# A slot order of its own for pair 5 in the RWKV-7 scan, with the value products and the output projection's first steps at other places

## The chip, the core and the metric

The kernel runs on one core of a Trainium2 chip. The metric is device time in microseconds (us) of one execution, the median of several. A core has five engines with an instruction queue each, and each queue runs strictly in its order: PE (TensorE, matrix products into PSUM banks), ACT (ScalarE), DVE (VectorE), POOL (GpSimd) and SP (SyncE), which here issues all DMA transfers. An instruction that waits for a semaphore holds up everything behind it in its queue.

## The reference, cut to what matters

The trunk has two layers on 512 tokens of 1024 channels. Each is a half-step SwiGLU FFN, a token mixer, and a second half-step FFN, each followed by a residual and a layer norm. Layer 0 mixes by neighbourhood attention, layer 1 by a bidirectional RWKV-7 scan. The change lies in that scan.

```python
def rwkv7_bidir(x, mix, w_rkv, ..., w_out):
    ...
    r = xr @ w_rkv[0]
    k = xk @ w_rkv[1]
    v = xv @ w_rkv[2]
    ...
    def step(state, inp):
        r_t, w_t, k_t, v_t, a_t, b_t = inp
        sa = jnp.einsum('zbhij,zbhj->zbhi', state, a_t)
        state = state * w_t[..., None, :] + sa[..., None] * b_t[..., None, :] + v_t[..., None] * k_t[..., None, :]
        return state, jnp.einsum('zbhij,zbhj->zbhi', state, r_t)

    _, ys = lax.scan(step, jnp.zeros((2, B, H, N, N), f32), xs)
    y = (ys[:, 0] + ys[::-1, 1]).transpose(1, 0, 2, 3)
    ...
    return ((y + bonus) * g).astype(x.dtype) @ w_out
```

There are 16 heads of 64 channels and two directions. The last line is the output projection: 512 x 1024 outputs, summed over 1024 channels. The layer adds `ALPHA * x` and normalises.

## The kernel before, in words

The scan treats two heads at a time: eight pairs, 0 to 7, of 128 channels each. A pair's sequence is cut in `NC` = 8 chunks of 64 tokens, and `chain` carries the state from chunk to chunk. One chunk takes four groups of small matmuls on PE with copies on other engines between them: `c` (line 1429), a copy to `wr` on ACT (1430), the first part of `y` (1433), `c` with `az` (1441), two copies to `vt` on ACT (1442, 1443), `m` (1447), and a product on DVE (1449) that gives the next chunk's `vt`. That chain of engines is serial; `outputs` (1460) and other pairs' work stand between its parts on PE.

Everything is written as Python generators, one per job and pair, and a program is made slot by slot: the slot of pair n runs `chain(n)`, and beside it the preparation of later pairs and the finishing of earlier ones. The order inside a slot is a string of letters in the table `SEQ`, one letter for one step of a generator; PE, ACT and DVE run in exactly the recorded order (`MANUAL_SCAN`). SP and POOL are ordered by the scheduler at build time, which places each DMA by its own estimate of when the DMA's waits end; on the chip that order is fixed. A slot without an entry of its own in `SEQ` takes entry 0; before the change, pair 5's slot did so. The letters that matter here:

- `c` chain, `d` outputs of the pair of the slot (5).
- `v` (`values`, line 1306): for pair n+2 = 7. The first step loads 512 KB of weights into the tile `wv`; the eight others each multiply one of 8 channel blocks of the activations `xv` with it into a bank "a" and after the eighth ACT copies the result. One such step is two matmuls (`wide`, line 990), which the profile shows as four records.
- `g0`, `g1` (`grams`): products of pair 7's tiles `ar` and `bk`, and DMAs that copy parts of `ar` into state tiles (`xs<-ar`, line 1292). `t0`, `t1` (`tails`, line 1302): transposes of `bk`.
- `k` (`inverted`, line 1380): pair 6's inverted blocks, a transpose on DVE and eight DMAs `az<-qd` (line 1385). `b` bonus; `x`, `e`, `n`, `j`, `i` other finishing and preparing steps.
- `o` (`outs`, line 1471): the output projection over the first `EARLY` = 5 channel blocks. It loads rows of `w_out`, 512 KB for a block, and the finished scan outputs of earlier pairs back from DRAM into `xv`, in place of the activations there. Then come 8 accumulations (4 token tiles x 2 column halves) of 5 steps each, so 40 steps. Each step is again one `wide`. The blocks of `w_out` have no room of their own: `w[0]` takes over `wv`, and `w[1]` to `w[4]` take over the two buffers of `ar` and the two of `bk`, oldest first, when pair 7 is done with them. `w[5]` to `w[7]` take over state tiles (line 1492 loads two of them).

Before, the `o` steps begin in the slot of pair 6, 26 of them, and 14 follow in the slot of pair 7. In the slot of pair 5 the last of the value steps stands almost at the slot's end.

Of the kernel before, what the change touches and what calls it, by code (L numbers as in the profile page):

```python
# [18 lines left out]
P = 128  # L19
# [23 lines left out]
CH = 64  # L43
NC = S // CH
# [940 lines left out]
class Scan:  # L985
# [485 lines left out]
    def outs(self):  # L1471

        nc = self.nc
        rows = lambda ap, k: ap[k * P : (k + 1) * P, :]
        w = [self.tile("wv", [P, ND, P]).rearrange("p a b -> p (a b)")]
        w += [self.tile(n, [P, NC, 2, CH], 2).rearrange("p a b c -> p (a b c)") for n in ("ar", "ar", "bk", "bk")]
        w += [self.units[i][0].rearrange("p a b c d -> p (a b c d)") for i in (2, 4, 3)]
        self.w, self.left = w, [rows(self.dram["x"], t) for t in range(NT)]
        for i in range(EARLY - 1):
            nc.sync.dma_start(self.xv[:, i, :], self.dram["o"][:, i, :])  # L1480
            nc.sync.dma_start(w[i], rows(self.w_out, i))
        for n, (t, h) in enumerate((t, h) for t in range(NT) for h in range(2)):
            hs = slice(h * 512, (h + 1) * 512)
            x = self.tile(("e", "e2", "th")[n % 3], [P, S], 2)
            nc.sync.dma_start(x, rows(self.dram["x"], t)[:, hs])
            acc = self.k.bank("ag"[n % 2])
            for i in range(EARLY):
                if n == 0 and i == EARLY - 1:
                    nc.sync.dma_start(self.xv[:, i, :], self.dram["o"][:, i, :])
                    nc.sync.dma_start(w[i], rows(self.w_out, i))  # L1490
                    for c in range(EARLY, ND - 1):
                        nc.sync.dma_start(w[c], rows(self.w_out, c))
                self.wide(acc, self.xv[:, i, t * P : (t + 1) * P], w[i][:, hs], i == 0, i == EARLY - 1)
                if i < EARLY - 1:
                    yield
            nc.vector.scalar_tensor_tensor(x, x, ALPHA, acc, ALU.mult, ALU.add)
            nc.sync.dma_start(rows(self.dram["x"], t)[:, hs], x)
            self.stored += 1
            self.reload()
            yield  # L1500
# [200 lines left out]
```

## Time and profile before

| what | value |
|---|---|
| median of three runs | 2250.02 us |
| lowest and highest run | 2245.41, 2254.24 us |
| the profiled execution's own time | 2249.58 us |
| its span, first to last instruction | 2247.8 us |
| mean granted clock of PE | 0.983 |

In the trace the slot of pair 5 lies from 1746.3 to 1784.0 us on PE, that of pair 6 to 1830.8, and that of pair 7 to 1857.4. A row of the timeline gives start and duration in us, engine, line, operation and tiles, the number of merged records, and in square brackets how long the engine had been idle and what released it. "SPq" rows are DMAs as SP issues them; when the data lands is in the DMA view. Records of PE are pipelined and overlap by some tens of ns.

### The profile page before, as it was taken

To read this page: it belongs to the slowest core of one execution; us is meant where nothing else is said; L and a number is where in the kernel's file an instruction comes from. 1 tells how busy PE (TensorE), PEld (TensorE's weight loads), DVE (VectorE), ACT (ScalarE), POOL (GpSimd) and SP (SyncE) were. 2 spreads that over 40 slices of the span, in tenths; PEclk is the share of its full clock that TensorE was granted. 3 is DMA by queue.
4 is the path that set the end of the run, shared out by engine and by line. 5 is a ranking of instruction groups with operands and counts; after the bars stand their busy time and mean duration, and the time that the engine had idled before them with its cause. 6 is when DMAs were issued, how large, how long until landed. Compare 5 with 4: busy or idle time off the path is not lost.

```text
span 2247.8 us, 35130 instructions
## 1 busy us (share of the span) xinstructions
PE 2169.0 (96%) x13784; PEld 1707.8 (76%) x13784; DVE 1068.3 (48%) x1549; ACT 973.8 (43%) x1706; POOL 1425.7 (63%) x1237
## 2 busy tenths in 40 slices
PE   8999999999999999999999988699999998999998
PEld 7888888887888888888888875435667656888886
DVE  2333356276423333743333698425778645232345
ACT  3333345376333333443333435336777633333333
POOL 6878855554487886588887433144776722888854
PEclk9999999999999999999999999799999999999999
DMA  6444463432344445354444534764454642544443
GB/s 199 143 145 145 143 229 97 135 89 91 103 141 150 145 141 174 132 181 137 141 141 132 196 123 155 268 162 117 126 137 111 206 149 94 159 141 141 141 169 122
DMA packets 350497, 328.82 MB, mean 146 GB/s; under 512 B 48458, under 2 KB 277450, under 8 KB 350332
## 3 DMA queue, kind: packets, MB, share of 16 engines
q1 hardware_dynamic: 350332, 326.58, 46.6%
q8 instruction: 108, 1.77, 0.3%
q14 instruction: 57, 0.47, 0.1%
HBM read 262.26 MB, written 47.74 MB: 138 GB/s over the span
## 4 chain that ended last, share of the span: by engine, by line
PE 83%; DVE 7%; DMA 4%; ACT 3%; issue 2%; POOL 1%; SPq 0%; DVEq 0%; ACTq 0%; POOLq 0%
PE bank L800 16%; PE bank L225 16%; PE bank L226 16%; PE bank L227 16%; PE bank L288 4%; PE a L990 3%; PE y L990 1%; PE g L1279 1%; DVE tmp L606 1%; PE m L990 1%; PE bank L1155 1%; DMA late<-in_ffn_w_out_dram 1%; PE g L990 1%; POOL w L221 1%; DMA wv<-in_w_rkv_dram 1%
## 5 line engine op out<-in xcount | busy, mean ns | idle before, releaser
L221 POOL TENSOR_TENSOR w<-raw,w 128x1024 fp32r<-128x1024 f32 (+2 forms) x203 | 507.2, 2500 | 248.3 <-ACT w L220 235.2
L226 PE MATMUL bank<-xT,w 128*128 128x512 f32 x1416 | 551.5, 389 | 1.7 <-DVE xT L221 1.7
L225 PE MATMUL bank<-xT,w 128*128 128x512 f32 x1416 | 552.5, 390 | 0.0
L227 PE MATMUL bank<-xT,w 128*128 128x512 f32 x1416 | 551.2, 389 | 0.0
L220 ACT ACTIVATE w<-raw 128x1024 fp32r<-128x1024 f32 x207 | 218.4, 1058 | 325.5 <-POOL ts L771 126.2
L422 DVE SCALAR_TENSOR_TENSOR ar<-bank,tmp 128x512 f32<-128x512 f32 x88 | 60.9, 692 | 585.1 <-PE bank L227 576.2
L226 PEld LDWEIGHTS bank<-xT,w 128*128 128x128 f32 x1416 | 265.9, 188 | 56.6 <-DVE xT L221 2.5
L227 PEld LDWEIGHTS bank<-xT,w 128*128 128x128 f32 x1416 | 265.8, 188 | 55.1
L225 PEld LDWEIGHTS bank<-xT,w 128*128 128x128 f32 x1416 | 265.9, 188 | 54.3
L1368 POOL TENSOR_TENSOR tm<-qs,zs 128x126 f32<-128x126 f32 (+22 forms) x248 | 104.9, 423 | 133.1 <-DVE qs L1361 83.9
L800 PE MATMUL bank<-wx,an 128*128 128x512 f32 x792 | 187.3, 389 | 0.0
L800 PEld LDWEIGHTS bank<-wx,an 128*128 128x128 f32 x792 | 148.7, 188 | 30.8
L800 PE MATMUL bank<-w,ring 128*128 128x512 f32 x720 | 168.8, 390 | 2.1 <-POOL w L221 2.1
L221 POOL TENSOR_TENSOR wx<-ra,wx 128x512 fp32r<-128x512 f32 x132 | 166.8, 1291 | 3.0 <-ACT wx L220 3.0
L221 DVE TENSOR_TENSOR ring<-ar,ring 128x1024 fp32r<-128x1024 f32 x44 | 122.8, 2792 | 81.3 <-ACT ring L220 81.2
L800 PEld LDWEIGHTS bank<-w,ring 128*128 128x128 f32 x720 | 134.9, 188 | 31.5 <-POOL w L221 3.2
L420 ACT ACTIVATE tmp<-bank 128x512 f32<-128x512 f32 x88 | 52.6, 598 | 231.0 <-PE bank L227 231.0
L221 POOL TENSOR_TENSOR ring<-raw,ring 128x1024 fp32r<-128x1024 f32 x28 | 68.2, 2445 | 96.7 <-ACT ring L220 96.6
L1370 POOL TENSOR_TENSOR zs<-zs,tm 128x126 f32<-128x126 f32 (+22 forms) x248 | 112.6, 454 | 19.4
L220 ACT ACTIVATE wx<-ra 128x512 fp32r<-128x512 f32 x132 | 82.9, 633 | 72.0 <-PE bank L800 67.8
L225 PE MATMUL bank<-xT,ring 128*128 128x256 f32 (+1 forms) x352 | 104.2, 304 | 9.8 <-ACT xT L220 3.7
L221 POOL TENSOR_TENSOR w<-late,w 128x1024 fp32r<-128x1024 f32 x30 | 75.6, 2525 | 58.8 <-ACT w L220 58.8
(284 smaller groups left out, 3779.0 us busy)
## 6 DMA issues: line engine op xcount, KB each, us to landing
raw<-in_ffn_w_in_dram SPq DMA_DIRECT2D x176, 512.0 KB, 3.9
ra<-in_ffn_w_out_dram SPq DMA_DIRECT2D x44, 1024.0 KB, 5.0
late<-d_late SPq DMA_DIRECT2D x34, 512.0 KB, 5.3
late<-in_ffn_w_out_dram SPq DMA_DIRECT2D x28, 512.0 KB, 4.6
raw<-in_w_qkv_dram SPq DMA_DIRECT2D x24, 512.0 KB, 3.9
d_late<-ts SPq DMA_DIRECT2D x44, 256.0 KB, 3.3
d_late<-ra SPq DMA_DIRECT2D x44, 256.0 KB, 2.0
xs<-ar SPq DMA_DIRECT2D x64, 128.0 KB, 2.4
```

Of the source, the lines that this page charges most:

```text
L220: self.hi = self.nc.scalar.activation(h, raw, AF.Copy).ins
L221: self.lo = (eng or self.nc.vector).tensor_tensor(l, raw, h.bitcast(F32), ALU.subtract).ins
L225: nc.tensor.matmul(out, wh, xh, start=start, stop=False)
L226: nc.tensor.matmul(out, wh, xl, start=False, stop=False)
L227: nc.tensor.matmul(out, wl, xh, start=False, stop=stop)
L288: nc.tensor.matmul(acc[t, h], a, u[:, i, h * 512 : (h + 1) * 512], start=first and n == 0, stop=last and n == 2)
L420: nc.scalar.activation(s, pg, AF.Silu)
L422: nc.vector.scalar_tensor_tensor(raw[:, 3:7:3] if j else raw[:, 0:8:7], halves_of(pu), 0.5, halves_of(s), ALU.mult, ALU.mult)
L800: self.nc.tensor.matmul(acc, lhs, u[:, i], start=bool(first) and m == 0, stop=last and m == 2, skip_group_check=more)
L990: self.nc.tensor.matmul(out[hs], w[:, hs], x, start=start, stop=stop)
L1368: nc.gpsimd.tensor_tensor(tv, qs[:, s, 0:s].rearrange("p (a o) -> p a o", o=1).broadcast_to([P, s, n]), zs[:, s : s + 1, c0:].broadcast_to ...
L1370: nc.gpsimd.tensor_tensor(zs[:, 0:s, c0:], zs[:, 0:s, c0:], tv, ALU.add)
```

## The change

Pair 5's slot gets an entry of its own in `SEQ`, and four `o` are taken out of pair 6's entry. Pair 5's entry is entry 0 without the letters that do nothing there (`l` and `f0`), with three of the `v` at earlier places, and with five `o` in the last quarter. `outs` has a new `yield` after its first four pairs of loads, so the first `o` records only loads and the next four are steps; and the order in which it takes over buffers is `ar`, `bk`, `ar`, `bk` in place of `ar`, `ar`, `bk`, `bk`.

```diff
-    6: "c x n c c x c c o c x c o d n o o o c o c c d c x o c o c x c c x d o c o c c c d o c n o o o o o c c d k c "
+    5: "c f1 x f1 v c n c f1 f1 v c g0 c c d v f1 c n c d g0 v c c g0 c x f1 v g0 c x x v n x t0 v c c v c d g0 c "
+       "g0 x g1 c c c g1 d g1 e v c g1 c c c d f1 t0 c t1 k g1 o k g1 i b c c d o c j c o d o c c t1 o c j b d",
+    6: "c x n c c x c c c x c d n o c o c c d c x o c o c x c c x d o c o c c c d o c n o o o o o c c d k c "
...
-        w += [self.tile(n, [P, NC, 2, CH], 2).rearrange("p a b c -> p (a b c)") for n in ("ar", "ar", "bk", "bk")]
+        w += [self.tile(n, [P, NC, 2, CH], 2).rearrange("p a b c -> p (a b c)") for n in ("ar", "bk", "ar", "bk")]
...
             nc.sync.dma_start(w[i], rows(self.w_out, i))
+        yield
```

The amount of work is the same: 40 `o` steps, of which 4 now stand in the slot of pair 5, 22 in that of pair 6 and 14 in that of pair 7. DVE and POOL keep their order entirely; ACT's order differs only in the place of the copy of pair 7's values. In the changed kernel all line numbers behind the table are higher by 2, and those behind the new `yield` by 3.

The order of SP (DMA issues) at the end of pair 5's slot, before. `bk_15802` is `w[3]`, `bk_15803` `w[4]`, `wv_15799` `w[0]` and `ar_15801` `w[2]`; `w[1]`, the other `ar`, was loaded some rows earlier:

```order
L1539 DMA d_o_82<-bon_15415 128x512
L1531 DMA gate_16200<-d_g_80 128x512
L1291 DMA az1_10806<-xs1_10796 64x4x64 x2
L1489 DMA xv_10776<-d_o_82 128x512
L1481 DMA bk_15802<-in_rw_out_dram 128x1024
L1385 DMA az0_10805<-qd_13994 32x8x32 x8
L1292 DMA xs1_10796<-ar_15167 64x512 x2
L1490 DMA bk_15803<-in_rw_out_dram 128x1024
L1481 DMA wv_15799<-in_rw_out_dram 128x1024
L1492 DMA xs2_10777<-in_rw_out_dram 128x1024
L1481 DMA ar_15801<-in_rw_out_dram 128x1024
L1492 DMA xs4_10779<-in_rw_out_dram 128x1024
```

The same place now, where `wv_15511`, `bk_15513`, `ar_15514` and `bk_15515` are `w[0]`, `w[2]`, `w[3]` and `w[4]`:

```order
L1483 DMA wv_15511<-in_rw_out_dram 128x1024
L1542 DMA d_o_82<-bon_15421 128x512
L1534 DMA gate_16200<-d_g_80 128x512
L1293 DMA az1_10806<-xs1_10796 64x4x64 x2
L1483 DMA bk_15513<-in_rw_out_dram 128x1024
L1492 DMA xv_10776<-d_o_82 128x512
L1387 DMA az0_10805<-qd_13994 32x8x32 x8
L1294 DMA xs1_10796<-ar_15167 64x512 x2
L1493 DMA bk_15515<-in_rw_out_dram 128x1024
L1495 DMA xs2_10777<-in_rw_out_dram 128x1024
L1495 DMA xs4_10779<-in_rw_out_dram 128x1024
L1483 DMA ar_15514<-in_rw_out_dram 128x1024
```

The load of `w[0]` has moved ahead of the eight `az<-qd`. Behind the last `xs1<-ar_15167`, which reads the buffer that `ar_15514` takes over, stand four loads of 512 KB now (five before), and `w[3]` is the last of them.

The order of PE at the end of the same slot, before (from the last two `y` of the last chunk; `xv,wv` is the last value step, `kz,onesb` the bonus; behind the last row pair 6's chain begins):

```order
L1433 MATMUL y_15122<-vt_14471,xs2_10777 64x64
L1433 MATMUL y_15122<-vt_14471,xs4_10779 64x64
L1302 MATMUL g_15691<-ident_58,bk_15168 128x128 x4
L990 MATMUL a_15177<-xv_10776,wv_15144 64x512 x2
L1441 MATMUL c_15679<-wr_15681,az2_10807 64x64 x4
L1408 MATMUL p_15706<-qd_13994,qc_13995 32x32 x32
L990 MATMUL a_15743<-kz_15174,onesb_10774 64x512 x2
L1460 MATMUL y_15122<-vt_14471,az2_10807 64x64 x4
```

And now:

```order
L1435 MATMUL y_15122<-vt_14471,xs2_10777 64x64
L1435 MATMUL y_15122<-vt_14471,xs4_10779 64x64
L1304 MATMUL g_15716<-ident_58,bk_15168 128x128 x4
L992 MATMUL a_15644<-ar_15514,xv_10776 64x512 x2
L1443 MATMUL c_15702<-wr_15704,az2_10807 64x64 x4
L1410 MATMUL p_15730<-qd_13994,qc_13995 32x32 x32
L992 MATMUL a_15767<-kz_15174,onesb_10774 64x512 x2
L1462 MATMUL y_15122<-vt_14471,az2_10807 64x64 x4
```

At the place of the last value step stands the fourth `o` step, which reads `w[3]` = `ar_15514`. The three other `o` steps stand within the two chunks before it, and three value steps stand in earlier chunks.

1 row of the table SEQ is left out of this document.

## The prediction

> **What bounds the kernel now.** I read the page first, then the stretches of the scan, then PE's waits in the slot of pair 5.
>
> ```profile
> span 2247.8 us, 35130 instructions
> ...
> PE 2169.0 (96%) x13784; PEld 1707.8 (76%) x13784; DVE 1068.3 (48%) x1549; ACT 973.8 (43%) x1706; POOL 1425.7 (63%) x1237
> ```
>
> PE is busy nearly all the time, so what is moved from one place of its queue to another gains only where it fills an idle stretch, and costs where PE is made to wait. The stretches of the slots of pairs 6, 5 and 7 (columns: length, then busy us of PE, PEld, DVE, ACT, POOL, then the granted clock):
>
> ```profile
> 1784.04:1830.75 46.71, 42.72 (x584) 23.61 (x582) 16.11 (x42) 14.19 (x39) 17.71 (x45) 0.96 0.52 168
> 1746.26:1784.04 37.78, 36.16 (x608) 25.51 (x604) 26.04 (x56) 26.18 (x73) 27.58 (x67) 1.00 0.66 192
> ```
>
> In pair 5's slot PE idles 1.6 us of 37.8, in pair 6's 4.0 of 46.7. What PE waited for in pair 5's slot:
>
> ```profile
> PE a L990 <- DMA wv<-in_w_rkv_dram: 0.7, 1, 0.7
> PE c L1429 <- DVE vt L1449: 0.5, 1, 0.5
> PE m L1447 <- ACT vt L1442: 0.3, 1, 0.3
> ```
>
> So work moved into this slot can hide in 0.8 us (the two waits of the chain); the 0.7 us comes before the first value product, whose place stays. The change must therefore earn its keep in pair 6's slot, and that depends on whether PE gets its operands in time. The rows of PE around the seam of the two slots:
>
> ```profile
> 1773.41 1.94 PE L990 MATMUL a<-xv,wv 128*64 128x512 f32 x8
> ...
> 1779.55 0.65 PE L1302 MATMUL g<-ident,bk 128*128 128x128 f32 x4
> 1780.13 1.08 PE L990 MATMUL a<-xv,wv 128*64 128x512 f32 x4
> ...
> 1787.75 1.01 PE L1429 MATMUL c<-vt,xs 128*64 128x64 f32 x8 [0.38 <-DVE vt L1449]
> 1788.89 1.98 PE L990 MATMUL a<-wv,xv 128*64 128x512 f32 x4
> ...
> 1797.29 0.71 PE L1429 MATMUL c<-vt,xs 128*64 128x64 f32 x7
> ```
>
> The row at 1780.13 is the last value step; the fourth `o` step takes its place. The chunk from 1787.75 to 1797.29 loses four `o` steps.
>
> **The change part by part.** *One step* costs 0.87 us of PE: in the next rows two steps follow each other (1.77 us from start to start), and a single one among other work takes as much.
>
> ```profile
> 1804.17 0.40 PE L1429 MATMUL c<-vt,xs 128*64 128x64 f32 x7
> ...
> 1807.49 1.94 PE L990 MATMUL a<-ar,xv 128*64 128x512 f32 x8
> 1809.26 1.89 PE L990 MATMUL a<-bk,xv 128*64 128x512 f32 x8
> ```
>
> *Until the fourth `o` step.* Three value steps come in earlier, the two at 1773.41 go out, three `o` steps come in: 4 x 0.87 = 3.5 us more before that place, less the 0.8 that the chain's waits cover. PE arrives at 1780.13 + 2.7 = 1782.8 in place of 1780.13; with no cover at 1783.6. On ACT the copy of the values comes earlier; ACT is busy 26.2 of 37.8 us there, so that is free. DVE and POOL keep their order.
>
> *The fourth step's operand.* This is where the argument turns. It reads `w[3]`, an `ar` buffer that the last two `xs<-ar` transfers still read, and SP is one queue in a fixed order. In the trace of before:
>
> ```profile
> 1776.35 5.91 SPq L1385 DMA_DIRECT2D az<-qd  x8
> 1782.36 1.20 SPq L1292 DMA_DIRECT2D xs<-ar  x2
> 1783.65 0.54 SPq L1490 DMA_DIRECT2D bk<-in_rw_out_dram  x1
> 1784.27 0.41 SPq L1481 DMA_DIRECT2D wv<-in_rw_out_dram  x1
> 1784.74 0.43 SPq L1492 DMA_DIRECT2D xs<-in_rw_out_dram  x1
> 1785.38 0.33 SPq L1481 DMA_DIRECT2D ar<-in_rw_out_dram  x1
> ```
>
> The eight `az<-qd` take SP 5.9 us, then come the two `xs<-ar`, and only then the big loads. In the changed order `w[3]` is the fourth of these (bk, xs, xs, ar), as the `ar` here is the fourth (bk, wv, xs, ar). When they land, from the DMA view (last column: us from issue to landing; the `ar` and the `xs` behind it in one answer, the `bk` alone, the small `xs<-ar` by their median):
>
> ```profile
> bk<-in_rw_out_dram SPq DMA_DIRECT2D x1, 512.0 KB, 3.9
> ```
>
> ```profile
> ar<-in_rw_out_dram SPq DMA_DIRECT2D x1, 512.0 KB, 7.5
> xs<-in_rw_out_dram SPq DMA_DIRECT2D x1, 512.0 KB, 8.3
> ```
>
> ```profile
> xs<-ar SPq DMA_DIRECT2D x6, 128.0 KB, 3.2
> ```
>
> The first landed at 1783.65 + 3.9 = 1787.6, the fourth at 1785.38 + 7.5 = 1792.9, 9.2 us after the first was issued. So the fourth load's landing is set by SP's queue and by the three loads ahead of it, not by PE. The start of the eight `az<-qd` follows a transpose on DVE:
>
> ```profile
> 1773.57 1.06 DVE L1380 STREAM_TRANSPOSE qd<-zs 128x512 f32<-128x512 f32 x1
> ```
>
> It stands behind the three value steps that came in (2.6 us, less the 0.8): it ends 1.8 later, at 1776.4. SP was not free before 1776.35, so the `az<-qd` move by 0 to 1.8 us; with SP still to issue two more transfers I take 0.6. Then the `ar` lands at 1793.5. Bounds: it cannot be issued before the `xs<-ar` have landed (1782.4 + 0.6 + 3.2 = 1786.2) and takes at least the 3.9 of a transfer with little ahead of it, so 1790.1; from above as long as the fifth load does here (1785.8 + 8.3 = 1794.1) with the full 1.8, so 1795.9. PE waits from 1782.8 to 1793.5, 10.7 us, with all of the end of the chain of pair 5 queued behind (its last `c<-wr,az`, the merge, the bonus, pair 6's first products), and ACT and DVE wait for those. The three `o` steps before it have loads further ahead in SP's queue; if one is a little late, that ends inside this wait. So the row at 1780.13 runs at 1793.5: **+13.4 us**. In the trace of before a first `o` step also waited for its load, but behind pair 5's chain and for the second of the loads (released at 1788.9).
>
> *The clock after the wait.* Columns as in the stretches above:
>
> ```profile
> 1784.00:1787.00 3.00, 1.68 (x32) 1.20 (x30) 2.36 (x6) 2.23 (x6) 2.56 (x6) 1.00 0.97 285
> ...
> 1788.00:1791.00 3.00, 2.88 (x20) 1.42 (x19) 1.76 (x7) 0.28 (x1) 2.59 (x6) 0.50 0.97 339
> ...
> 1458.00:1463.00 5.00, 5.00 (x14) 1.30 (x14) 0.98 (x2) 0.00 (x0) 0.00 (x0) 0.50 1.08 355
> ```
>
> Already 1.3 us of idleness in three brought the granted clock to 0.50 here for some 3 us; and at the start of the scan, after a wait, it stayed there for 5 us of full work:
>
> ```profile
> 1457.79 6.38 PE L990 MATMUL y<-az,xs 128*64 128x512 f32 x16 [3.94 <-DMA xs<-in_w_rkv_dram]
> ...
> 1466.10 1.89 PE L990 MATMUL y<-xs,xs 128*64 128x512 f32 x8
> ```
>
> Sixteen records in 6.38 us against 2 x 1.89 at full clock: 2.6 us lost. After a wait of 10 us I take these **+2.6**; at least 0. [...]
>
> *Pair 6's slot.* The chunk from 1787.75 to 1797.29 took 9.5 us. Without the four steps it holds the rows from 1804.17 to 1807.49 (a chunk with one `o` step and the transposes) and one step more: 3.3 + 0.9 = 4.2. That is 5.3 less: 3.5 for the steps and 1.8 for the wait on `wv` and the half clock. But the idle stretches just ahead (1784 to 1787) are those of the chain itself and come again; if the clock drops again, a chunk at half speed for 3.3 us gives back 1.7. Nothing says which; I take the middle, **-4.5**.
>
> The sum: 13.4 + 2.6 - 4.5 = **+11.5 us**. The profiled execution took 2249.58 us (1.8 more than its span), so 2261.1; it lies 0.4 below the median of the runs, which would make 2261.5. I say **2261 us**. Behind this place both kernels do the same work in the same order, with PE as the bound, so the shift should last to the end.
>
> **The rivals.** *The load is in time, and the steps are hidden* (the other side: not slower). Then PE runs through: +2.7 before the seam, -5.3 behind it, so -2.6, 2247 us. It decides at a landing before 1780.13 + 5.3 = 1785.4. For it: three value steps come earlier, so `wv` and `xv` come free earlier, and those loads do move ahead in SP's queue. Against it: the `w[3]` load does not, and its lower bound is 1790.1. 10%.
>
> *The wait, but no slow clock*: 13.4 - 5.3 = +8.1, 2258 us. Against it: the clock fell after much less idleness. 12%.
>
> *A later landing*: the fourth load at its upper bound, 1795.9, with the clock down twice: 15.8 + 2.6 - 3.6 = +14.8, 2264 us. For it: DMA was at 0.97 of its engines' time in 1784 to 1791, so anything more in the queues shows at once. 22%.
>
> *That something behind absorbs it*: of the 4.0 us that PE idled in pair 6's slot 1.3 lie at its head, in the row of 1784 to 1787. If the other 2.7 fell away, 2258 us; I give it no case of its own but let the range hold it.
>
> **How the numbers follow.** The forecast has 54%, with a range of its own from 2257 to 2265; the three rivals 10, 12 and 22%, the rest is unknown. About 0.5% (11.3 us) is what a measurement of this kernel can tell from no change: the three runs lie within 0.4%. The bound above is 2261.3, and the forecast stands on it: half of its chance (0.27) and the later landing (0.22) lie above, 0.49 together. Faster by 0.5% would need -11, four times what the hidden case gives: 0.05, from the unknown and a little of that case. The rest, 0.46, is no change. The range from 2252 to 2267 leaves out the hidden case and little more.
>
> **What would show it.** Right: in the profile of the changed kernel PE has one wait of 8 to 13 us ahead of `a<-ar,xv` at the end of pair 5's slot, released by the DMA `ar<-in_rw_out_dram`; that load is issued behind two `xs<-in_rw_out_dram`; the granted clock is 0.5 right behind it; and pair 6's chunk with the transposes of `v` takes 4 to 6 us in place of 9.5. Wrong: if this wait is under 4 us, the whole sign turns; if it is 10 us but the span grows by less than 5, a slack behind the scan took it, and PE's idle time after 1860 will be smaller than before by as much.

## The result, and the profile after

| | before | after |
|---|---|---|
| median, us | 2252.01 (4 runs) | 2268.76 (4 runs) |
| lowest and highest, us | 2245.41, 2254.24 | 2266.21, 2271.40 |
| the profiled execution's own time, us | 2249.58 | 2266.21 |
| its span, us | 2247.8 | 2264.4 |
| mean granted clock of PE | 0.983 | 0.977 |

The ratio is 1.0075, with an interval of 95% from 1.0053 to 1.0097: the change costs 16.8 us between the medians, where 11.5 was forecast, and the time lies just above the range. (In the diff of "The change" two letters of entry 5 are swapped: the kernel that ran has `o c j c o d c o c t1 o c j b d` there. The rows of the order are those of the kernel that ran.)

The head of the page of the changed kernel, with the busy times as in the prediction:

```profile
span 2264.4 us, 35129 instructions
...
PE 2175.9 (96%) x13784; PEld 1712.2 (76%) x13784; DVE 1079.1 (48%) x1549; ACT 973.8 (43%) x1706; POOL 1421.6 (63%) x1237
```

PE does the same 13784 matrix instructions, and yet is busy 6.9 us longer, with a mean granted clock of 0.977 in place of 0.983; the other 9.7 us of the 16.6 are idleness. So two things are to be looked for: waits, and half clock. The stretches of the slots of pairs 5 and 6 (columns: length, busy us of PE, PEld, DVE, ACT, POOL, then granted clock, DMA share, GB/s):

```profile
1741.89:1799.88 57.99, 46.65 (x624) 28.92 (x620) 26.15 (x56) 26.56 (x73) 42.91 (x107) 0.81 0.60 177
1799.88:1846.80 46.92, 42.47 (x567) 24.87 (x567) 15.12 (x42) 13.93 (x38) 1.44 (x6) 0.84 0.38 124
```

Pair 5's slot went from 37.78 to 57.99 us, +20.2. Pair 6's, which was to give 4.5 back, kept its length (46.71 to 46.92). Their clock fell from 1.00 and 0.96 to 0.81 and 0.84. So the two slots cost 20.4 us in this execution; it had come to the slot of pair 5 4.4 us ahead (1741.89 against 1746.26), with nothing changed before it. That looks like chance: in the executions profiled here that point lies up to 12 us apart. PE's three longest waits from 1735 to 1885 (what waited, what released it, us in total, times, longest):

```profile
PE a L992 <- DMA ar<-in_rw_out_dram: 7.6, 1, 7.6
PE a L992 <- DMA wv<-in_rw_out_dram: 2.8, 1, 2.8
PE p L1410 <- issue: 2.8, 1, 2.8
```

Where the waits stand on PE:

```profile
1771.67 0.45 PE L1462 MATMUL y<-vt,az 64*64 64x64 f32 x8
1774.91 1.98 PE L992 MATMUL a<-wv,xv 128*64 128x512 f32 x4 [2.79 <-DMA wv<-in_rw_out_dram]
...
1779.78 1.92 PE L992 MATMUL a<-ar,xv 128*64 128x512 f32 x4
...
1784.69 0.66 PE L1304 MATMUL g<-ident,bk 128*128 128x128 f32 x4
1792.97 1.98 PE L992 MATMUL a<-ar,xv 128*64 128x512 f32 x4 [7.63 <-DMA ar<-in_rw_out_dram]
```

The row at 1792.97 is the fourth `o` step, and it waits for `ar`, as predicted. The first `o` step, at 1774.91, waits too. An `o` step takes 1.9 to 2.0 us here where it took 1.08 in the slot of pair 6: half clock. The clock, by stretches:

```profile
1775.00:1778.00 3.00, 3.00 (x36) 1.27 (x38) 0.00 (x0) 0.35 (x2) 2.32 (x9) 0.50 0.97 252
...
1781.00:1784.00 3.00, 3.00 (x22) 1.46 (x22) 0.00 (x0) 0.28 (x1) 2.48 (x7) 0.50 0.52 112
...
1793.00:1797.00 4.00, 4.00 (x68) 2.27 (x70) 0.00 (x0) 0.54 (x2) 3.37 (x9) 0.50 0.00 1
...
1804.00:1807.00 3.00, 2.62 (x39) 2.16 (x37) 2.11 (x8) 0.64 (x3) 0.00 (x0) 0.50 0.06 20
...
1810.00:1815.00 5.00, 5.00 (x90) 3.37 (x88) 2.65 (x11) 1.10 (x4) 0.00 (x0) 1.00 0.30 108
```

It is 0.50 for the 9 us behind the first wait, and again for 14 us behind the second. SP's queue at the same place:

```profile
1768.69 0.58 SPq L1483 DMA_DIRECT2D wv<-in_rw_out_dram  x1
1769.32 0.47 SPq L1542 DMA_DIRECT2D d_o<-bon  x1
...
1775.55 0.33 SPq L1492 DMA_DIRECT2D xv<-d_o  x1
1775.96 5.24 SPq L1387 DMA_DIRECT2D az<-qd  x8
1781.30 1.19 SPq L1294 DMA_DIRECT2D xs<-ar  x2
1785.38 0.34 SPq L1493 DMA_DIRECT2D bk<-in_rw_out_dram  x1
1785.77 0.90 SPq L1495 DMA_DIRECT2D xs<-in_rw_out_dram  x2
1786.77 0.36 SPq L1483 DMA_DIRECT2D ar<-in_rw_out_dram  x1
```

The `ar` load is the fourth of the big loads, behind the eight `az<-qd`, the two `xs<-ar`, one `bk` and two `xs`. Counted from PE's first `c` of the slot, the `az<-qd` start at 34.1 us; before, they started at 1776.35 - 1746.26 = 30.1. That is 4.0 later. Two of SP's longest waits there name what held it, and the third row, of the kernel before, shows that one of them was there already:

```profile
SPq L1493 <- PE g L1304: 2.8, 1, 2.8
SPq L1492 <- DMA d_o<-bon: 2.6, 1, 2.6
```

```profile
SPq L1489 <- DMA d_o<-bon: 1.4, 1, 1.4
```

SP holds the eight small transfers up because a load of `xv` ahead of them (the block for the fifth `o` step) reads what `d_o<-bon` has just written. The rows of before:

```profile
1770.51 0.54 SPq L1539 DMA_DIRECT2D d_o<-bon  x1
...
1774.70 0.33 SPq L1489 DMA_DIRECT2D xv<-d_o  x1
```

`d_o<-bon` was issued 24.3 us into the slot before, and is issued at 27.4 now; and it takes longer. Of the DMA view (last column: us from issue to landing) first the row of before, then that of the changed kernel:

```profile
d_o<-bon SPq DMA_DIRECT2D x1, 256.0 KB, 4.1
```

```profile
d_o<-bon SPq DMA_DIRECT2D x1, 256.0 KB, 6.2
```

Two 512 KB loads now fly beside it that did not before: `wv`, issued just ahead of it, and `bk`, just behind. With SP's order of before it takes 4.1 us, and with the early loads 6.2 in the changed kernel and 5.6 to 6.0 in kernels 1, 2, 4 and 5 below. That fits the loads' traffic as the cause; no kernel takes away one of them alone.

The other wait, of 2.8 us, is that of the first big load, `bk`: it takes over a buffer that PE's transposes at 1784.69 still read, and these stand behind the first wait and its half clock.

### The profile page after: what moved, and what is told of

The parts are those of the page before. It is cut to its first block, busy times and chain, and to the rows that moved or that the text cites. A ratio compares the mean times of both kernels' runs of the same rounds, so it can differ in the third digit from the quotient of the medians.

```text
span 2264.4 us, 35129 instructions
## 1 busy us (share of the span) xinstructions
PE 2175.9 (96%) x13784; PEld 1712.2 (76%) x13784; DVE 1079.1 (48%) x1549; ACT 973.8 (43%) x1706; POOL 1421.6 (63%) x1237
## 5 line engine op out<-in xcount | busy, mean ns | idle before, releaser
L223 POOL TENSOR_TENSOR w<-raw,w 128x1024 fp32r<-128x1024 f32 (+2 forms) x203 | 501.0, 2469 | 253.3 <-ACT w L222 240.5
L223 DVE TENSOR_TENSOR ring<-ar,ring 128x1024 fp32r<-128x1024 f32 x44 | 133.2, 3027 | 74.5 <-ACT ring L222 74.4
```

Source lines behind the costliest of these rows:

```text
L223: self.lo = (eng or self.nc.vector).tensor_tensor(l, raw, h.bitcast(F32), ALU.subtract).ins
```

## The experiments

All were timed in rounds beside the kernel before, and the ratio is to that. Every profile quoted is of the kernel named.

| kernel | median, us | ratio | interval of 95% |
|---|---|---|---|
| the change | 2268.76 | 1.0075 | 1.0053 to 1.0097 |
| 1: fourth `o` step back in pair 6's slot | 2253.28 | 1.0017 | 1.0007 to 1.0027 |
| 2: all four steps back | 2253.32 | 1.0012 | 1.0001 to 1.0024 |
| 3: `ar` first of the four loads | 2263.22 | 1.0065 | 1.0049 to 1.0080 |
| 4: the three steps later | 2267.23 | 1.0067 | 1.0051 to 1.0083 |
| 5: as 4, the `xv` load out of the way | 2264.80 | 1.0061 | 1.0048 to 1.0075 |
| 6: nine wide products in the wait | 2257.91 | 1.0036 | 1.0023 to 1.0048 |
| 7: 18 tiny products in the wait | 2262.54 | 1.0045 | 1.0028 to 1.0063 |
| 8: before, 18 tiny products in pair 6's slot | 2253.78 | 1.0012 | 1.0000 to 1.0024 |
| 9: before, 18 tiny products at the scan's head | 2250.88 | 1.0003 | 0.9990 to 1.0016 |
| 10: three steps, each in time | 2250.94 | 0.9995 | 0.9984 to 1.0006 |
| 11: as 10, with 16 tiny products | 2254.26 | 1.0008 | 0.9996 to 1.0020 |
| 12: as 1, first step reads an earlier load | 2253.64 | 1.0014 | 1.0005 to 1.0023 |

**1. The fourth step alone.** It goes back to pair 6's slot; nothing else moves.

```diff
-       "g0 x g1 c c c g1 d g1 e v c g1 c c c d f1 t0 c t1 k g1 o k g1 i b c c d o c j c o d c o c t1 o c j b d",
-    6: "c x n c c x c c c x c d n o c o c c d c x o c o c x c c x d o c o c c c d o c n o o o o o c c d k c "
+       "g0 x g1 c c c g1 d g1 e v c g1 c c c d f1 t0 c t1 k g1 o k g1 i b c c d o c j c o d c o c t1 c j b d",
+    6: "c x n c c x c c c x c d n o o c o c c d c x o c o c x c c x d o c o c c c d o c n o o o o o c c d k c "
```

> The change with three steps in place of four in pair 5's slot: the fourth, which waits for the ar load, goes back to pair 6's slot. SP's order is that of the change. Theory A (the loss is the two waits for loads of w_out, 2.8 and 7.6 us in the profile of the change, and the half clock behind each of them): the 7.6 us wait and the slow stretch behind it go, the 2.8 us wait on wv and its slow stretch stay; about 2257 us (2252 to 2260), 9 to 16 below the change. Theory B (the earlier value steps and loads cost by themselves, the waits only move): still above 2263.

Measured: 2253.28, as A expected. One step at that place is worth 0.0058 of the time, some 13 us, most of what the change costs. Some 4 of these us lie elsewhere: in the last chunk of pair 6's slot, where PE stops (`issue`), the two profiles are 3.8 us apart. The slot of pair 5 is 44.0 us (counted by ACT's first copy to `wr` in each slot: 37.8 before, 58.3 in the changed kernel).

**2. The early loads and value steps alone.** Entry 5 keeps only the `o` that loads, and entry 6 is that of before.

```diff
-       "g0 x g1 c c c g1 d g1 e v c g1 c c c d f1 t0 c t1 k g1 o k g1 i b c c d o c j c o d c o c t1 o c j b d",
+       "g0 x g1 c c c g1 d g1 e v c g1 c c c d f1 t0 c t1 k g1 o k g1 i b c c d c j c d c c t1 c j b d",
```

> The change with the values and the loads moved, but all four steps back in pair 6's slot at their places of before. Theory A: no wait in pair 5's slot, and wv has landed when pair 6's slot asks for it; 2251 us (2247 to 2254), the same as before or a little less. Theory B: above 2258.

Measured: 2253.32 and a ratio of 1.0012, inside A's range, though not "the same as before or a little less". So the value steps and early loads cost some 3 us by themselves (0 to 5 by the interval; a part of it may be the stop late in pair 6's slot, whose chunk takes 11.2 us in this profile and 8.2 before), and gain nothing: pair 5's slot grows by 1.8 us and does not shrink where the value steps went out. I put that down to the chain: PE's longest wait for a copy to `wr` is 1.6 us in this profile, and 0.2 in the changed kernel's.

**3. The `ar` load first.** The loads recorded at the fifth step are held behind that of `w[3]`.

```diff
-            nc.sync.dma_start(w[i], rows(self.w_out, i))
+            first = nc.sync.dma_start(w[i], rows(self.w_out, i)).ins
...
-                    nc.sync.dma_start(w[i], rows(self.w_out, i))
-                    for c in range(EARLY, ND - 1):
-                        nc.sync.dma_start(w[c], rows(self.w_out, c))
+                    with self.k.behind(first):
+                        nc.sync.dma_start(w[i], rows(self.w_out, i))
+                        for c in range(EARLY, ND - 1):
+                            nc.sync.dma_start(w[c], rows(self.w_out, c))
```

> The change with the load of w[3] (ar) held ahead of the other three large loads in SP's queue; PE's order is that of the change. Theory A (three loads ahead of it set when it lands): it can go out when the xs<-ar have landed and then lands some 3 us earlier, 1789.5 in place of 1793.0 in the time of the change's profile: the wait is 4 to 5 us, the clock still falls, 2265 us (2262 to 2267). Theory D (the wait is set by the xs<-ar ahead and the load's own time, the order of the four does not matter): 2268 to 2269.

Measured: 2263.22, inside A's range; but the interval of its ratio overlaps that of the change, so the time alone does not show a gain. PE and SP in its profile:

```profile
1750.01 0.45 PE L1431 MATMUL c<-vt,xs 128*64 128x64 f32 x8
...
1796.13 1.98 PE L992 MATMUL a<-ar,xv 128*64 128x512 f32 x4 [6.44 <-DMA ar<-in_rw_out_dram]
```

```profile
1792.43 0.34 SPq L1483 DMA_DIRECT2D ar<-in_rw_out_dram  x1
```

The wait was to be 4 to 5 us and is 6.4, because PE comes earlier too (its first wait is 1.7 us in place of 2.8). The fourth step runs 46.1 us into the slot, in place of 51.1. In both kernels SP is done with the two `xs<-ar` at 40.6 us, so these 5.0 us belong to the place among the four loads: the `ar` load no longer stands behind `bk`, which waits for PE, and it lands 3.7 us after its issue in place of 6.2. The prediction had that place in its sum, though not the wait of `bk`; the rest of the lateness lies ahead of all four.

**4. No first wait.** The three steps come later in the slot, so that `wv` has landed.

```diff
-       "g0 x g1 c c c g1 d g1 e v c g1 c c c d f1 t0 c t1 k g1 o k g1 i b c c d o c j c o d c o c t1 o c j b d",
+       "g0 x g1 c c c g1 d g1 e v c g1 c c c d f1 t0 c t1 k g1 o k g1 i b c c d c j c o d c o c o t1 o c j b d",
```

> The first three o steps of pair 5's slot come two to three chunk parts later, so that w[0] has landed when PE reaches the first of them; on SP the ar load is still the last of the four. Theory A (the text of the prediction: a wait before the fourth step ends inside the wait on ar, and is free): the wait of 2.8 us on wv goes, the wait on ar grows to 9 to 11 us, the row of the fourth step stays within 1 us of its place relative to the slot's start, and the time stays at 2267 to 2270. Theory B (the wait on wv is paid: the half clock behind it delays the transposes of bk, and with them the loads behind them on SP): the half clock of 1775 to 1784 goes, ar lands 2 to 3 us earlier, and the time is 2263 to 2266.

Measured: 2267.23, as A expected. PE from the profile of this kernel:

```profile
1744.71 0.45 PE L1431 MATMUL c<-vt,xs 128*64 128x64 f32 x8
...
1794.83 1.98 PE L992 MATMUL a<-ar,xv 128*64 128x512 f32 x4 [10.00 <-DMA ar<-in_rw_out_dram]
```

The wait on `wv` is gone, the wait on `ar` is 10.0, and the fourth step stands 50.1 us into the slot, in place of 51.1. So the first wait and its half clock end inside the second but for 1.0 us, nearly as the prediction said. Here `bk` is the third of the loads and SP no longer waits for PE; SP is late all the same.

**5. The `xv` load out of the way.** As 4, and the load of `xv` that waits for `d_o<-bon` goes behind the eight `az<-qd` (`azl` is the last of them) and the two `xs<-ar`.

```diff
-                    nc.sync.dma_start(self.xv[:, i, :], self.dram["o"][:, i, :])
+                    with self.k.behind(self.azl):
+                        nc.sync.dma_start(self.xv[:, i, :], self.dram["o"][:, i, :])
```

> As the run with the three o steps later (2267.2 us), and besides the load of the fifth block of xv, which waits on SP for d_o<-bon, goes behind the eight az<-qd and the two xs<-ar; the ar load then is the third of the four big loads. Theory A (what makes ar late beyond the prediction is SP itself: the xv load waits 2.5 us for d_o<-bon and holds the eight az<-qd): the az<-qd start 2.5 us earlier relative to the slot's start (31 in place of 33.8 us), ar lands 3 to 4 us earlier (46 in place of 49.6), the wait on ar falls to 6 to 7 us, and the time is 2262 to 2265. Theory B (ar's landing is set by PE's and DVE's own progress, the transposes and the zs transpose): the az<-qd start at 33 or later, and the time stays at 2266 to 2268.

Measured: 2264.80, inside A's range; by the ratios it does not stand clear of kernel 4, and the wait (8.5 us) and the landing are later than A had them. What it shows is in the rows. Three of its PE and SP:

```profile
1744.94 0.45 PE L1431 MATMUL c<-vt,xs 128*64 128x64 f32 x8
...
1792.54 1.97 PE L992 MATMUL a<-ar,xv 128*64 128x512 f32 x4 [8.47 <-DMA ar<-in_rw_out_dram]
```

```profile
1775.28 7.79 SPq L1387 DMA_DIRECT2D az<-qd  x8
```

The `az<-qd` start 30.3 us into the slot (34.3 in kernel 4), and the fourth step runs at 47.6 in place of 50.1. So the load of `xv` on the queue makes `ar` late. The eight transfers took 7.8 us in place of 6.2, and so 1.5 of the 4.0 were lost again.

**6. The clock kept up.** Nine wide products into a bank that nothing reads run on PE inside the wait, ahead of the fourth step.

```diff
+                if n == 0 and i in WARM:
+                    idle = self.k.bank("g")
+                    for _ in range(WARM[i]):
+                        self.wide(idle, self.onesb, self.ah[:, 0, :].bitcast(F32), True, True)
```

> The change, with nine products of no use (two matmuls of 512 columns each, about 7.8 us together) on PE right ahead of the step that waits 7.6 us for the ar load; SP's order is that of the change. They keep PE busy in the wait and end about when the load lands. Theory A: the granted clock is 1.0 behind the wait in place of 0.50 from 1793 to 1807, worth 5 to 6 us: 2263 us (2260 to 2266). Theory C (the wait alone counts, the clock costs at most the 2.6 us of the prediction): 2266 to 2270.

Measured: 2257.91, 11 us under the changed kernel (9 by the ratios) and below what either theory expected. The same 172 matrix records, from the fourth step's start to the first step of the next accumulation (`g<-wv,xv`, in pair 6's slot), first in the changed kernel and then here:

```profile
1792.97:1809.21 16.24, 14.54 (x172) 9.16 (x174) 4.69 (x15) 6.43 (x17) 7.10 (x22) 0.53 0.10 34
```

```profile
1792.61:1803.57 10.96, 9.26 (x172) 5.80 (x174) 4.93 (x15) 6.39 (x17) 9.03 (x25) 1.00 0.13 50
```

The half clock behind the wait costs 5.3 us. PE waited for `ar` here for 2.4 us behind the nine products, and the clock stayed at 1.00. The gain was larger than 5.3 because two more things went. One is the stop at line 1410 (`issue`), late in pair 6's slot, whose chunk takes 5.9 us in place of 11.4. The other is the half clock behind the first wait: PE waited 2.0 us there, and in this execution the clock did not fall.

```profile
1775.00:1784.00 9.00, 7.97 (x132) 4.26 (x134) 2.44 (x4) 3.16 (x8) 6.23 (x19) 1.00 0.71 174
```

The transposes of `bk` came 5.6 us behind the start of the first step then, in place of 9.8, and the fourth step ran 48.7 us into the slot in place of 51.1. The three, 5.3, 5.5 and 2.4, are what the two slots are shorter by, 13.2 us.

**7. The stop alone.** 18 tiny products (64x8) in the same place: as many instructions, little work.

```diff
+                if n == 0 and i == 3:
+                    idle = self.k.bank("g")
+                    for _ in range(TINY):
+                        self.nc.tensor.matmul(idle[A, :8], self.onesb[:, A], self.onesb[:, :8], start=True, stop=True)
```

> The changed kernel with 18 very small products (64x8 outputs, into a bank that nothing reads) on PE ahead of the fourth o step; they run inside the wait on ar, too short to keep PE busy. All other queues keep their order. It separates the two things that nine wide products did at once in the run before: filling the wait, and putting 18 instructions ahead of the place at the end of pair 6's slot where PE stops for 2 to 3 us with no releaser shown. Theory S (the stop hangs on the position in PE's instruction stream): it is gone, the half clock behind it too, and the time falls by 3 to 5 us, to 2264 to 2266; the waits on wv and ar stay at 2.8 and 7 to 8 us. Theory C (it came from the clock and the timing of the transfers): the stop stays at 2 to 3 us and the time at 2267 to 2270.

Measured: 2262.54, between the two kernels and below the range of S. The slow stretch behind the wait is there as before:

```profile
1789.10:1805.38 16.28, 14.58 (x172) 9.19 (x174) 4.73 (x15) 6.47 (x17) 8.90 (x26) 0.53 0.10 33
```

and the stop is gone: the last chunk of pair 6's slot takes 5.9 us (11.4 in the changed kernel, 8.2 before). That fits S, and the fall of 6 us (the intervals of the ratios overlap) is near the 5.5 that this chunk lost. The waits did not stay quite as they were, 1.9 and 5.6 us in this profile, and the fourth step ran 1.5 us earlier in the slot.

**8 and 9. The stop in the kernel before.** 18 tiny products, in 8 ahead of the fourth accumulation in pair 6's slot, in 9 at the head of the scan, where PE waits anyway (8.2 us in the kernel before), some 380 us earlier.

```diff
+                if n == 3 and i == 0:
+                    idle = self.k.bank("g")
+                    for _ in range(TINY):
+                        self.nc.tensor.matmul(idle[A, :8], self.onesb[:, A], self.onesb[:, :8], start=True, stop=True)
```

```diff
+        if hp == z == 0:
+            idle = k.bank("g")
+            for _ in range(TINY):
+                nc.tensor.matmul(idle[A, :8], self.tri[:, 0, A], self.tri[:, 0, :8], start=True, stop=True)
```

> The kernel before with 18 very small products on PE in pair 6's slot, ahead of the third accumulation's successor (the fourth), where no wait stands; all other queues keep their order. Theory S: the stop of 2.2 us at the end of that slot is gone or sits elsewhere, and the time falls by 1 to 3 us, to 2247 to 2249. Theory C: the stop stays, and the time is 0 to 1.5 us longer by the 18 products.

> The kernel before with 18 very small products at the head of the scan, where PE waits for the mask; they shift all later PE instructions by 36 records. Theory S (the stop hangs on the position in PE's instruction stream): it moves 36 records ahead or goes, and the time is 0 to 3 us shorter, 2247 to 2251. Theory C (it hangs on what else goes on at that time, such as the transfers): it stays at the same two records, the last of the merge, at 2 us, and the time is unchanged.

Measured: 2253.78 and 2250.88; no gain in either. PE's rows of the stop in the kernel before, and in 9:

```profile
1823.12 1.19 PE L1408 MATMUL p<-qd,qc 32*32 32x32 f32 x63
1826.49 0.18 PE L1408 MATMUL p<-qd,qc 32*32 32x32 f32 x1 [2.17 <-issue]
```

```profile
1820.00 0.62 PE L1413 MATMUL p<-qd,qc 32*32 32x32 f32 x27
1822.22 0.76 PE L1413 MATMUL p<-qd,qc 32*32 32x32 f32 x37 [1.59 <-issue]
```

The stop came behind 63 of the 64 products of the merge, and comes behind 27 in 9, and in 8 too: 36 records earlier, and 18 products make 36 records. So in these two it moved with the place in PE's instruction stream, as S expected; putting products in moved it and did not remove it.

**10. Three steps, each in time.** As 1, with the three steps later.

```diff
-       "g0 x g1 c c c g1 d g1 e v c g1 c c c d f1 t0 c t1 k g1 o k g1 i b c c d o c j c o d c o c t1 c j b d",
+       "g0 x g1 c c c g1 d g1 e v c g1 c c c d f1 t0 c t1 k g1 o k g1 i b c c d c j c o d o c o c t1 c j b d",
```

> Three o steps in pair 5's slot as in the first experiment (the fourth back in pair 6's), each one place later, so that w[0] has landed. Theory A (waits on operands are what the change costs; without them the steps fill idle time of the chain): no wait on wv, the slot of pair 5 2 to 4 us shorter than with three steps at their old places (44.0), and the time 2248 to 2251, no slower than before. Theory B (three more steps cost their PE time wherever they stand in this slot): the slot stays at 42 to 44 us and the time at 2252 to 2255.

Measured: 2250.94, a ratio of 0.9995 with 1 inside its interval: as fast as before, and faster than the change. By the time A was right, but not by its way: pair 5's slot took 43.6 us, hardly less than the 44.0 of kernel 1. No load is waited for, but PE waits 1.6 us for a copy of ACT's (line 1432). Behind the same wait in kernel 4 the granted clock was 0.70 from 1778 to 1781 and 0.73 from 1781 to 1784.

**11. The same, with the stop moved.** A further yield in `outs` and 16 tiny products behind it, for which entry 5 has one more `o`.

```diff
-       "g0 x g1 c c c g1 d g1 e v c g1 c c c d f1 t0 c t1 k g1 o k g1 i b c c d c j c o d o c o c t1 c j b d",
+       "g0 x g1 c c c g1 d g1 e v c g1 c c c d f1 t0 c t1 k g1 o k g1 i b c c d o c j c o d o c o c t1 c j b d",
...
+        yield
+        idle = self.k.bank("g")
+        for _ in range(TINY):
+            nc.tensor.matmul(idle[A, :8], self.onesb[:, A], self.onesb[:, :8], start=True, stop=True)
```

> The kernel with three o steps, each in time (2250.9 us), with 16 very small products on PE in the idle gap of 1.6 us in the last chunks of pair 5's slot. Theory S (the stop late in pair 6's slot hangs on where PE's instruction blocks are fetched; products put in far ahead shift it away, as in the two runs where it was gone): no stop, the last chunk of pair 6's slot 6 in place of 10 us, and the time 2246 to 2249, below the kernel before. Theory C (products that are put in only move the stop by as many records, as in the kernel before with 18): a stop of 1.5 to 3 us stays, and the time is 2250 to 2252.

Measured: 2254.26, no gain. The stop moved (behind 30 of 64 products, 1.5 us), and a second of 1.6 us came up in pair 5's slot, ahead of a product of line 1404.

**12. An earlier load for the first step.** As 1, but `w[0]` is an `ar` buffer and `w[1]` is `wv`.

```diff
-        w = [self.tile("wv", [P, ND, P]).rearrange("p a b -> p (a b)")]
-        w += [self.tile(n, [P, NC, 2, CH], 2).rearrange("p a b c -> p (a b c)") for n in ("ar", "bk", "ar", "bk")]
+        w = [self.tile(n, [P, NC, 2, CH], 2).rearrange("p a b c -> p (a b c)") for n in ("ar", "bk", "ar", "bk")]
+        w.insert(1, self.tile("wv", [P, ND, P]).rearrange("p a b -> p (a b)"))
```

> As the run with three o steps in pair 5's slot (2253.3 us; the first of them waits 2.0 us for wv), but w[0] takes over an ar buffer and w[1] takes wv, so that the first step reads the load that SP issues some 2 us earlier. SP keeps its order. Theory A (the place is good, only its operand is late: PE there has an idle gap of 1.6 us that a step can fill): no wait on a load over 1 us, full clock behind it, pair 5's slot 41 to 42.5 us in place of 44.0, and the time 2248 to 2251. Theory B (the time goes by the sum of PE's work and by the stop late in pair 6's slot): the slot falls by under 1 us and the time stays at 2251 to 2254.

Measured: 2253.64, the time of B by the way of A. The first step waits for nothing, and the slot falls from 44.0 to 41.3 us. But PE now comes earlier to the next loads. Its waits:

```profile
PE a L992 <- DMA ar<-in_rw_out_dram: 2.2, 1, 2.2
PE a L992 <- DMA bk<-in_rw_out_dram: 1.5, 1, 1.5
```

The fourth step waits 2.2 us for the same late `ar`, now in pair 6's slot, whose second chunk takes 10.6 us (5.1 in kernel 1). The landing of that load limits what this kernel can gain from earlier steps.

## Why the prediction was wrong

The direction, the place and the releaser were right; the time lay 7.8 us above the forecast and 1.8 above the range; some 2 us of the 7.8 are the kernel before, whose median rose from 2250.02 to 2252.01 with a fourth run. Term by term, in the profiled execution:

| term | forecast | measured |
|---|---|---|
| the row at 1780.13, later in the slot by | +13.4 | +17.2 |
| half clock behind that wait | +2.6, and 0.8 in the next | +5.3 |
| pair 6's slot without the four steps | -4.5 (-5.3 at full clock) | -5.3 |
| the stop and its clock at the end of pair 6's slot | none | +3.2 |
| both slots | +11.5 | +20.4 |

The third row is what remains: from the fourth step's place to the end of pair 6's second chunk (by ACT's copies to `wr`) both kernels take 18 us, so the 5.3 of half clock and the gain of the steps cancel.

*The fourth step's operand.* The wait was to be 10.7 us for one load. It was 7.6 there (under the 8 to 13 that were named as the sign) and 2.8 ahead of the first step, 10.4 together. The sentence that "if one is a little late, that ends inside this wait" nearly held: kernel 4 takes the first wait away and wins 1.0 us of the fourth step's place. The step that failed is "I take 0.6" for how far the eight `az<-qd` move on SP, bounded by 0 and 1.8. They moved by 4.0. That bound counted only what DVE hands to SP. It left out the load of `xv` that stands ahead of them and waits for `d_o<-bon`, which was in the trace of before with 1.4 us. It also priced nothing for the early `wv` load, though the two orders show it going ahead of `d_o<-bon`. That transfer was issued 3.2 us later in the slot (1.8 of it by the longer chunks that took in the value steps, counted by ACT's copies to `wr`) and took 2.1 longer; the load of `xv` waited for it, and the small transfers stood behind. Kernel 5 shows the hold: without that load ahead the `az<-qd` start 4.0 earlier, and the fourth step runs 2.5 earlier. The landing was set "not by PE", the prediction says; that failed too, by the 1.0 us of kernel 4, as `bk` waited for PE's transposes. The landing forecast was 47.2 us into the slot (1793.5 - 1746.26); kernel 5, without either hold, has 47.6, though with longer small transfers.

*The clock.* The mechanism was right, its size was not. 2.6 us came from one row at the start of the scan, and 0.8 more from taking the middle in pair 6's slot; kernel 6 measures 5.3. The half clock outlasted the 5 us taken for it: it held for some 14 us, of which PE was busy for 12.3, as the chain of pair 6 begins there; and behind the first wait it stayed at 0.50 for 9 us with PE wholly busy by the profile.

*Pair 6's slot.* The chunk with the transposes of `v` was to take 4 to 6 us in place of 9.5; it took 5.6. The gain came, and was lost again at the slot's end: the stop of 2.2 us before became 2.8, and half clock followed it. These two rows read that clock, in the changed kernel and before, where no half clock followed:

```profile
1840.00:1845.00 5.00, 5.00 (x26) 1.86 (x26) 0.55 (x1) 2.04 (x6) 0.00 (x0) 0.50 0.73 218
```

```profile
1826.49:1831.49 5.00, 4.89 (x49) 2.39 (x48) 2.19 (x4) 2.86 (x8) 0.00 (x0) 1.00 0.74 215
```

The prediction had no term for this: the stop was among the 2.7 us of idleness in that slot which it left alone. Whether the loss belongs to the change is not settled. The stop is in both kernels, and kernel 7, without it, is 6 us faster. Its length does not decide alone: half clock followed stops of 1.9 to 2.5 us in the profiles of kernels 2, 3, 5 and 10 (the first `o` step behind them took 1.65 to 1.97 us, against 1.08 at full clock), and not the 2.2 of before. The wait of the fourth step does not either, since kernel 2 has no `o` step in pair 5's slot at all.

*The rivals.* "The load is in time" was off by far: `ar` landed 7.6 us after PE came. "The wait, but no slow clock" was priced at +8.1; kernel 6, which keeps the clock and lacks the stop, is 8.1 us above before by its ratio (0.0036 of 2250). That agreement is partly luck, since it lacks the stop, which before had with 2.2 us. "A later landing" was the nearest: it put the landing at 1795.9 less 1746.26, 49.6 us into the slot, and 51.1 was measured, but by another way than the one given for it. "That something behind absorbs it" did not come about: from the end of pair 6's slot to the end, both kernels take 417 to 418 us.

*The sum.* The two slots lost 20.4 us in the profiled execution and the medians are 16.8 apart, whose interval is 12 to 22; the 4.4 by which that execution was ahead covers the difference. The range was too narrow above: it took in the bounds of the landing and the clock singly, with the landing's upper bound (49.6 us into the slot) set too low, and it had no term for the stop.

## What to carry to other kernels

Behind a load that was moved ahead on the queue, with another one close by, a transfer took 6.2 us in place of 4.1: look at who waits in the queue for such a transfer, before putting a step at the place that hangs on the queue's last load. Waits that are already in the queue's trace belong in the sum. Putting the load that is waited for first among its neighbours brought it in 5.0 us earlier (kernel 3). A step that waits in an otherwise full PE queue cost its wait and then, in half clock behind it, 5.3 us more; the row at full work had given 2.6. And taking away the nearest wait helped only up to the next load that was late (2.2 us for `ar` in kernel 12): look for the landing that bounds all of them.

## What the runs showed of the hardware

**The clock.** It fell to 0.50 behind a wait of 2.8 us and stayed there for 9 us of full work, and again behind one of 7.6 us, for 14 us, of which PE was busy for 12.3; behind a wait of 2.4 us that followed 8 us of wide products (kernel 6) it did not fall. Among the waits of 1.6 to 2.8 us the length did not decide: behind 1.6 us it was 0.70 in kernel 4 (1778 to 1781), and behind 2.0 in kernel 1 an `o` step took 1.80 us, against 1.08 at full clock, while behind 2.0 in kernel 6 and 2.2 in the kernel before it stayed at 1.00.

**The stop called "issue".** It falls together with a packet on the queue that the profile names `q8 instruction`; that PE waits for this packet is an inference from the times. In the DMA view of the changed kernel the stretches 1814 to 1822.5 and 1837.5 to 1838.5 have these rows (queue, packets, MB, share of the engines), and the 15 us between them have none of that queue:

```profile
q8 instruction: 2, 0.03, 1.5%
```

```profile
q8 instruction: 1, 0.02, 6.0%
```

Then PE goes on:

```profile
1835.97 1.19 PE L1410 MATMUL p<-qd,qc 32*32 32x32 f32 x63
1839.92 0.26 PE L1410 MATMUL p<-qd,qc 32*32 32x32 f32 x1 [2.75 <-issue]
```

PE stops at 1837.17, and the packet comes at 1837.5; in the kernel before one comes at 1824.0, and PE stops from 1824.3 to 1826.5. The queue moved 108 packets in the whole execution, one for every 255 records of PE and PEld in the mean; that they are PE's instructions is my guess and was not shown. Here 554 such records passed between two packets, and the like gap stands ahead of the stop in the kernel before (542). At this one place the stop cost 1.4 to 2.8 us in the kernels that have it and, in the changed kernel and some others, the clock behind it. Why PE stops there, and why it did not in kernels 6 and 7, stays open.
